# A transformer layer whose instruction order comes from a list scheduler in the kernel's source instead of hand-set slots

## The chip, the cores and the metric

The kernel runs on one core of a Trainium2 chip. The metric is the device time of one execution in microseconds (us), as the median of several runs. A core has TensorE (PE, matrix products; its weight loads are shown as PEld), VectorE (DVE), ScalarE (ACT), GpSimd (POOL) and SyncE (SP), whose queue issues most transfers here. Each engine works through its own queue in order. An instruction waits at the head of its queue until what it needs has come from the other engines, and everything behind it waits too. So the order in which the kernel's source emits instructions is the order in which each engine runs them.

## The reference

One layer, all in float32, with 512 tokens, width 2048, and 16 heads of 128 columns:

```
h    = RMSNorm(x)
proj = h @ w_in                      # 2048 x 8192: qA kA vA gA qB kB vB gB, 1024 columns each
A (8 heads): stick-breaking attention, strictly causal, weights from exp, log and a running sum
B (8 heads): softmax over the chunk itself and all chunks before it, normed q and k, bias by distance
mixed = concat(yA * silu(gA), yB * silu(gB))
x     = x + mixed @ w_out            # 2048 x 2048
```

## The kernel before

*Products.* Each matrix product is split twice. Every float32 operand is written as a high part plus a low part of a shorter format (`wh`, `wl` for weights, `xh`, `xl` for activations), and three matmuls (`three`, L217 to L219) give high x high, high x low and low x high. On top of that, a 2 x 2 scheme of blocks with seven products instead of eight (the names in `ORDER`: A11, A12, s3, A22, s2, s1, s4) is used; the operands' sums are made beforehand and the results are put together afterwards by `combine`.

*Units and steps.* The projection is 32 units (`u`). Four units make a group `g` of two heads: q, k, v and the gates. Even groups belong to attention A, odd ones to B. A unit has 4 steps, each with 7 products of 6 matmuls. The output product has 4 quarters of 512 columns, each with 8 steps, and a step has 7 products of 3 matmuls for each of two halves of the tokens (`a`). So there are 160 steps of 42 matmuls. The first eight steps alternate between units 0 and 1.

*What a step needs.* `load` issues two transfers of 256 KB for its weights (three buffers `wt`), `add` makes the sums on VectorE (L145 to L147: 512, 256 and 256 columns), `split` casts the high part on ScalarE (L157) and subtracts for the low part on VectorE (L159), in two parts of 1,024 and 768 columns with two buffers each. The activations go the same way in eight blocks `j` (`x_load`, `x_scale`, `x_sums` at L199 to L202, `x_split` with L210 and L213): once at the start for x, and once more for the mixed heads ahead of the output product. Their staging buffers are the pairs (`cq`, `ck`) and (`cv`, `cg`), which otherwise hold a group's q, k, v and gates.

*PSUM.* It has eight banks of 512 columns, and each product takes half a bank. The units go round five of the banks; banks 5, 6 and 7 (`SPARE`) serve the attention. `combine` reads a unit's seven products (L275 on ScalarE; L278, L279, L281, L282, L284 on VectorE) into `c`, or in the output stage into `co`. It has one scratch buffer `U`. In the output stage the halves `a` use banks 0 to 3 and 4 to 7.

*Attention.* For each head: `prep_a`, or `forth` and `back`, prepare q and k; `score` makes the scores of four blocks of tokens; `turn` transposes the weights (L574); `v_turn` transposes v (L601); `values` multiplies and then, with the head's gates, stores the mixed head to DRAM (`mixd`, L640). `gates` applies SiLU (L647), which needs a table to be loaded. `rstd` and `R` hold the row norms of x, made from sums of squares over `xs` (L316).

*What sets the order.* Time in the source is counted in slots, one for each product of a projection step. `at(slot, fn)` enters a job, `run(slot)` emits all that are due. A job is a generator whose `yield 1.5` means that it goes on 1.5 slots later; `TO_PE` (4 slots) and `TO_OTHER` (1.5) are the lags put between one engine's work and the next one's. `plan(g)` enters a group's jobs at fixed slots after the end of its units. The main loop emits the products in order, calling `run` between them, and the four parts of `combine` directly behind the second, fifth, sixth and seventh product of a unit's last step:

```
run(s0 + p - 0.5)
product(n, name)
if last and p in (1, 4, 5, 6):
...
    next(cg_, None)
run(s0 + p)
```

*Residual.* At the end of each quarter and half, two transfers bring the block of x (`xres`, L774), VectorE adds it to `co` (L780), and two transfers write the result (L782).

Of the kernel before, what the change touches and what calls it, by code (L numbers as in the profile page):

```python
# [14 lines left out]
P = 128  # L15
# [31 lines left out]
def trunk_kernel(ctx: ExitStack, tc: tile.TileContext, xT, xn, wi, wqk, wo, ng, qg, kg, rel, out):  # L47
# [55 lines left out]

    sequence = list(range(NU))
# [19 lines left out]

    wt_, whl = {}, {}

    def load(n):
        if n >= NS:
            return
# [10 lines left out]
    def add(n):  # L140

        if n >= NS:
            return
        t = wt_[n]
        dve.tensor_tensor(out=some(t, 8, -7, 2), in0=some(t, 5, -5, 2), in1=some(t, 1, 0, 2), op=ALU.add)  # L145
        dve.tensor_tensor(out=some(t, 9, 2), in0=some(t, 8, 2), in1=some(t, 0, 2), op=ALU.add)  # L146
        dve.tensor_tensor(out=some(t, 12, 1), in0=some(t, 9, 2), in1=some(t, 4, 2), op=ALU.add)  # L147

    def split(n, part):

        if n >= NS:
            return
        t = wt_[n][:, (0, 8 * P)[part]:(8 * P, 14 * P)[part]]
        w = (8 * P, 6 * P)[part]
        h, l = (tmp([P, w], f"{x}{part}", f"{x}{part}_{n}", F32R, bufs=2) for x in ("wh", "wl"))
        whl[n, part] = h, l
        act.copy(h, t)  # L157
        yield 1.5
        dve.tensor_tensor(out=l, in0=t, in1=h.bitcast(F32), op=ALU.subtract)  # L159
# [13 lines left out]
    stage = {}  # L173

    def x_load(j, mixed, tags):
        r = tmp([P, 4 * H], tags[0], f"xr{j}{mixed}")
        t = tmp([P, 4 * H], tags[1], f"xt{j}{mixed}")
        stage[j] = r, t
        if mixed:
            for tag in tags:  # L180
                emptied(tag, NG - 1)
        if mixed:
            a, b = mixd[NJ + j], mixd[j]
        else:
            a, b = xT[:, j, :], xT[:, j + NJ, :]
        sp.dma_start(r[:, :H], a[:, :H])
        sp.dma_start(r[:, H:3 * H], b)
        sp.dma_start(r[:, 3 * H:], a[:, H:])

    def x_scale(j):  # L190
        r, _ = stage[j]
        a, b = ng_t[:, j:j + 1], ng_t[:, j + NJ:j + NJ + 1]
        for s_, g_ in ((slice(0, H), a), (slice(3 * H, 4 * H), a), (slice(H, 3 * H), b)):
            act.activation(r[:, s_], r[:, s_], AF.Copy, scale=g_)

    def x_sums(j, eng):
        r, t = stage[j]
        two = lambda x: x.rearrange("p (a b) -> p a b", b=H)
        eng.tensor_tensor(out=two(t[:, :2 * H]), in0=r[:, None, 3 * H:].to_broadcast([P, 2, H]),  # L199
                          in1=two(r)[:, 0:3:2, :], op=ALU.subtract)  # L200
        eng.tensor_tensor(out=t[:, 2 * H:3 * H], in0=t[:, :H], in1=r[:, 2 * H:3 * H], op=ALU.subtract)
        eng.tensor_tensor(out=t[:, 3 * H:], in0=t[:, 2 * H:3 * H], in1=r[:, H:2 * H], op=ALU.add)  # L202

    def x_split(j):
        r, t = stage.pop(j)
# [3 lines left out]
        for src, a, b in ((r[:, :3 * H], 0, 3), (t, 3, 7)):  # L209
            act.copy(f(h[:, a:b]), src)  # L210
        yield 1
        for src, a, b in ((r[:, :3 * H], 0, 3), (t, 3, 7)):
            dve.tensor_tensor(out=f(l[:, a:b]), in0=src, in1=f(h[:, a:b]).bitcast(F32), op=ALU.subtract)  # L213
# [20 lines left out]

    def product(n, name, a=0):
        u, r = steps_[n]
        if u < NU:
            o = halves[:, place(unit_banks(u), name), :]
# [7 lines left out]
        else:  # L246
            o = halves[:, place((4 * a, None), name), :]
# [3 lines left out]
                  r == NJ - 1, skip_group_check=True)  # L251

# [18 lines left out]
    def combine(b, c, ut):  # L271


        u = ut.rearrange("p (a b) -> p a b", b=H)
        act.copy(u, pair(b, "A11", "A12"))  # L275
        yield
        c = c()
        dve.tensor_tensor(out=c[0][:, 1, :], in0=one(b, "s2"), in1=u[:, 0, :], op=ALU.add)  # L278
        dve.tensor_tensor(out=c[0][:, 0, :], in0=u[:, 0, :], in1=u[:, 1, :], op=ALU.add)  # L279
        yield  # L280
        dve.tensor_tensor(out=u, in0=pair(b, "s3", "s1"), in1=twice(c[0][:, 1, :]), op=ALU.subtract)  # L281
        dve.tensor_tensor(out=c[1], in0=pair(b, "A22", "s1"), in1=twice(u[:, 0, :]), op=ALU.add)  # L282
        yield
        dve.tensor_tensor(out=c[0][:, 1, :], in0=one(b, "s4"), in1=u[:, 1, :], op=ALU.subtract)  # L284

    def emptied(tag, g):

        n = head(g, 1)
        k = ("cq", "ck", "cv", "cg").index(tag)
        last = (("prep", n, 0), ("prep", n, 1), ("v", g, 1) if g < NG - 2 else ("mix", g, 1), ("mix", g, 1))[k]  # L290
        assert g < 0 or last in done, (tag, g)

    def result(u):
        emptied(("cq", "ck", "cv", "cg")[u % 4], u // 4 - 1)
        C[u // 4, u % 4] = t = tmp([P, 2, S], ("cq", "ck", "cv", "cg")[u % 4], f"c{u}")
        t = t.rearrange("p a (b c) -> p a b c", c=H)
        return [t[:, 0], t[:, 1]]


    def rsqrt(v, y, n):  # L300

        w = nwt[:, :n]
        act.activation(w, v, AF.Ln)
        act.activation(y, w, AF.Exp, scale=-0.5)
        yield 1
        dve.tensor_tensor(out=w, in0=y, in1=y, op=ALU.mult)
        dve.tensor_tensor(out=w, in0=w, in1=v, op=ALU.mult)
        dve.tensor_scalar(out=w, in0=w, scalar1=-0.5, scalar2=1.5, op0=ALU.mult, op1=ALU.add)
        dve.tensor_tensor(out=y, in0=y, in1=w, op=ALU.mult)

    def x_stats(t, i):
        k, = yield from buffer("W")
        x_ = tmp([P, S], "W", "xs", bufs=3)
        sp.dma_start(x_, xn[t][:, i * S:(i + 1) * S])
        yield 7
        act.activation(x_, x_, AF.Square, accum_out=ssx[:, t * 4 + i:t * 4 + i + 1])  # L316
# [3 lines left out]
    def x_rstd():  # L320
        yield from until(lambda: all(("stat", t, i) in done for t in range(NT) for i in range(4)))
        dve.tensor_reduce(out=vx, in_=ssx.rearrange("p (a b) -> p a b", b=4), axis=mybir.AxisListType.X, op=ALU.add)
        dve.tensor_scalar(out=vx, in0=vx, scalar1=1.0 / D, scalar2=EPS, op0=ALU.mult, op1=ALU.add)
        yield 1
        yield from rsqrt(vx, rstd, NT)
        dve.tensor_tensor(out=rstd2, in0=rstd, in1=rstd, op=ALU.mult)
        yield from x_spread()

    def x_spread():
# [4 lines left out]
        pool.memset(o, 1.0)  # L334
        for t in range(NT):
            dve.tensor_scalar(out=d[:, t * P:(t + 1) * P], in0=ident, scalar1=rstd[:, t:t + 1], scalar2=None, op0=ALU.mult)
        yield 2
        for t in range(NT):
            s_ = slice(t * P, (t + 1) * P)
# [481 lines left out]
```

## Time and profile before

| | |
|---|---|
| median of 3 runs | 1125.21 us (1120.92 to 1125.61) |
| the profiled execution | 1127.8 us, span 1126.0 us |
| busy: PE / DVE / ACT / POOL | 981.1 / 895.8 / 582.8 / 8.3 us |
| granted TensorE clock, mean | 0.961 |
| matmuls | 7,496, of which 6,720 are the 160 steps' |
| bytes moved | 112.42 MB, 100 GB/s over the span |

Busy time is the union of an engine's instructions. Matmuls overlap one another, and their ends are modelled, so a busy PE may still do less than it can; counting the matmuls that start in a stretch is safer. In a table of windows, each row is a stretch of the span with its length, and for each engine the busy time and the number of instructions; then the granted clock (PEclk, 1 is full speed), the share of the DMA engines' time, and GB/s. A row of waits has who waited, for whom, then the total in us, the number of waits, and the longest. A row of the timeline has start and duration in us, engine, source line, operation, result and sources, and in brackets the engine's idle time before it with what ended that.

### The profile page before, as it was taken

To read this page: it belongs to the slowest core of one execution; us is meant where nothing else is said; L and a number is where in the kernel's file an instruction comes from. 1 tells how busy PE (TensorE), PEld (TensorE's weight loads), DVE (VectorE), ACT (ScalarE), POOL (GpSimd) and SP (SyncE) were. 2 spreads that over 40 slices of the span, in tenths; PEclk is the share of its full clock that TensorE was granted. 3 is DMA by queue.
4 is the path that set the end of the run, shared out by engine and by line. 5 is a ranking of instruction groups with operands and counts; after the bars stand their busy time and mean duration, and the time that the engine had idled before them with its cause. 6 is when DMAs were issued, how large, how long until landed. Compare 5 with 4: busy or idle time off the path is not lost. (4 is left out here: it accounts for less than half of the span.)

```text
span 1126.0 us, 19319 instructions
## 1 busy us (share of the span) xinstructions
PE 981.1 (87%) x7496; PEld 945.5 (84%) x7496; DVE 895.8 (80%) x1541; ACT 582.8 (52%) x1073; POOL 8.3 (1%) x49
## 2 busy tenths in 40 slices
PE   4678879999998899999899999998998888797986
PEld 4568879998998899889889998898898887697986
DVE  6778968787887878888878887887778799867775
ACT  5665654465365545653655565455556454332331
POOL 0000000000000000000000000000000000000000
PEclk9789999999998999999899999999899999899998
DMA  4462223222222322223223222322123244434341
GB/s 149 147 204 80 76 66 112 92 88 85 85 76 76 94 86 94 85 85 103 64 77 115 95 86 83 104 76 85 58 75 103 85 134 143 146 115 147 110 153 57
DMA packets 63884, 112.42 MB, mean 100 GB/s; under 512 B 7472, under 2 KB 11568, under 8 KB 63792
## 3 DMA queue, kind: packets, MB, share of 16 engines
q1 hardware_dynamic: 63792, 111.19, 30.9%
q8 instruction: 58, 0.95, 0.4%
q14 instruction: 34, 0.28, 0.1%
HBM read 102.77 MB, written 8.39 MB: 99 GB/s over the span
## 5 line engine op out<-in xcount | busy, mean ns | idle before, releaser
L217 PE MATMUL banks<-xh,wh 128*128 128x256 f32 x1792 | 528.6, 295 | 44.5 <-DVE c L278 21.0
L219 PE MATMUL banks<-xh,wl 128*128 128x256 f32 x1792 | 518.7, 289 | 35.8 <-DVE wl L159 35.7
L218 PE MATMUL banks<-xl,wh 128*128 128x256 f32 x1792 | 515.8, 288 | 1.1 <-DVE xl L213 1.1
L157 ACT CAST wh<-wt 128x1024 fp32r<-128x1024 f32 (+1 forms) x320 | 295.1, 940 | 365.0 <-DVE wt L147 124.1
L159 DVE TENSOR_TENSOR wl<-wt,wh 128x1024 fp32r<-128x1024 f32 (+1 forms) x320 | 343.8, 1088 | 106.4 <-ACT wh L157 105.7
L217 PEld LDWEIGHTS banks<-xh,wh 128*128 128x128 f32 x1792 | 352.8, 197 | 53.9 <-DVE c L278 27.3
L219 PEld LDWEIGHTS banks<-xh,wl 128*128 128x128 f32 x1792 | 352.4, 197 | 41.2 <-DVE wl L159 41.2
L218 PEld LDWEIGHTS banks<-xl,wh 128*128 128x128 f32 x1792 | 352.5, 197 | 1.8 <-DVE xl L213 1.4
L217 PE MATMUL banks<-wh,xh 128*128 128x256 f32 x448 | 131.6, 294 | 18.3 <-DVE co L278 9.7
L218 PE MATMUL banks<-wl,xh 128*128 128x256 f32 x448 | 132.4, 296 | 7.5 <-DVE wl L159 7.5
L219 PE MATMUL banks<-wh,xl 128*128 128x256 f32 x448 | 131.6, 294 | 3.2 <-DVE xl L213 3.2
L145 DVE TENSOR_TENSOR wt<-wt 128x512 f32<-128x512 f32 x160 | 109.5, 684 | 0.0
L217 PEld LDWEIGHTS banks<-wh,xh 128*128 128x128 f32 x448 | 89.8, 200 | 20.7 <-DVE co L278 11.4
L218 PEld LDWEIGHTS banks<-wl,xh 128*128 128x128 f32 x448 | 89.8, 201 | 10.5 <-DVE wl L159 10.5
L219 PEld LDWEIGHTS banks<-wh,xl 128*128 128x128 f32 x448 | 90.0, 201 | 5.3 <-DVE xl L213 5.2
L146 DVE TENSOR_TENSOR wt<-wt 128x256 f32<-128x256 f32 x160 | 68.0, 425 | 5.5
L147 DVE TENSOR_TENSOR wt<-wt 128x256 f32<-128x256 f32 x160 | 68.1, 425 | 5.5
L574 PE MATMUL banks<-ident,W 128*128 128x128 f32 x160 | 30.1, 288 | 12.9 <-DVE wtl L582 5.3
L275 ACT COPY U<-banks 128x512 f32<-128x512 f32 x40 | 23.5, 588 | 31.5 <-PE banks L219 21.3
L580 ACT CAST wth<-banks 128x128 fp32r<-128x128 f32 (+1 forms) x64 | 26.8, 423 | 22.0 <-PE banks L574 22.0
L281 DVE TENSOR_TENSOR U<-banks,c 128x512 f32<-128x512 f32 x32 | 22.1, 690 | 19.6 <-PE banks L219 19.6
L582 DVE TENSOR_TENSOR wtl<-banks,wth 128x128 fp32r<-128x128 f32 (+1 forms) x64 | 30.6, 483 | 7.1 <-ACT wth L580 7.0
(112 smaller groups left out, 902.7 us busy)
## 6 DMA issues: line engine op xcount, KB each, us to landing
wt<-in_wi SPq DMA_DIRECT2D x256, 256.0 KB, 3.0
wt<-in_wo SPq DMA_DIRECT2D x64, 256.0 KB, 3.1
xs<-in_xn SPq DMA_DIRECT2D x16, 256.0 KB, 4.0
mixd<-c SPq DMA_DIRECT2D x16, 256.0 KB, 2.1
xres<-in_xn SPq DMA_DIRECT2D x16, 256.0 KB, 3.9
out<-xres SPq DMA_DIRECT2D x16, 256.0 KB, 2.6
xr<-in_xT SPq DMA_DIRECT2D x16, 128.0 KB, 3.5
xr<-in_xT SPq DMA_DIRECT2D x8, 256.0 KB, 3.8
```

The source lines that it names most:

```text
L145: dve.tensor_tensor(out=some(t, 8, -7, 2), in0=some(t, 5, -5, 2), in1=some(t, 1, 0, 2), op=ALU.add)
L146: dve.tensor_tensor(out=some(t, 9, 2), in0=some(t, 8, 2), in1=some(t, 0, 2), op=ALU.add)
L147: dve.tensor_tensor(out=some(t, 12, 1), in0=some(t, 9, 2), in1=some(t, 4, 2), op=ALU.add)
L157: act.copy(h, t)
L159: dve.tensor_tensor(out=l, in0=t, in1=h.bitcast(F32), op=ALU.subtract)
L217: pe.matmul(o, lh, rh, start=start, stop=False, **kw)
L218: pe.matmul(o, lh, rl, start=False, stop=False, **kw)
L219: pe.matmul(o, ll, rh, start=False, stop=stop, **kw)
L275: act.copy(u, pair(b, "A11", "A12"))
L574: pe.transpose(t[:, j * P:(j + 1) * P], src[:, j * P:(j + 1) * P], ident)
L580: act.copy(th[:, blocks, :], tv)
L582: dve.tensor_tensor(out=tl[:, blocks, :], in0=tv, in1=th[:, blocks, :].bitcast(F32), op=ALU.subtract)
```

## The change

The slots, lags and the loop over them are removed. In their place a list scheduler runs while the kernel's source is executed. It keeps a clock of its own and a queue of ready operations for each engine. An operation has an engine, a cost (constants such as 0.075 us + 1.04 ns for each column on VectorE), and a due time. Each job is a generator that yields either an operation, which is made ready when its inputs are finished by that clock (0.06 us later, or 0.4 us for TensorE), or a condition to wait for. When an engine is free, the ready operation with the earliest due time is emitted. TensorE takes ready attention work first and the next product of the steps (0.705 or 0.355 us) otherwise, when the weights' split, the activations and the bank are there. The operations for weights and activations are due a few us ahead of the product that uses them (`need`). Loads have a bandwidth of 330 GB/s and a latency of 2.2 us in this model.

```diff
+    def issue(engine, op):
+        op.fn()
+        busy[engine] = clock[0] + op.cost
...
+    def schedule(next_product):
...
+            for e in ready:
+                if busy[e] > clock[0] + 1e-9:
+                    continue
+                if ready[e]:
+                    k = min(ready[e], key=lambda k: (k[0].due(), k[3]))
...
+                elif e == "PE":
+                    op = next_product()
...
+    def sums(n, k0, k1):
...
+        yield DV(512, lambda: dve.tensor_tensor(out=some(t, 8, -7, 2), ...), need(k0, 4))
+        spawn(split(n, 0, k0), (0, n))
...
+        yield AC(w, hi, need(k, 2.6))
+        h, l = x
+        yield DV(w, lambda: dve.tensor_tensor(out=l, in0=t, in1=h.bitcast(F32), op=ALU.subtract), need(k, 0.5))
...
-    def give(i, wait=3.0):
-        yield wait * LAG[0]
+    def give(i):
         del owner[i]
-    LAG = [1.0]
-    TO_PE, TO_OTHER = 4.0, 1.5
```

The transfers and operations are the same but for these points. The mixed activations' block `j` is staged in (`cq`, `ck`) where `j` is even and in (`cv`, `cg`) where it is odd, each block after the one before it in its pair; before, blocks 0 to 3 all used (`cq`, `ck`). `cv` comes free when the last group's heads are mixed, `cg` when the second of them is stored:

```diff
+        tags = STAGE[j % 2]
...
+            yield lambda: (("store", g, j % 2) in done and ("store", g + 1, j % 2) in done
+                           and all(emptied(t_, NG - 1) for t_ in tags)
+                           and position[0] >= at_step[steps_.index((last, j // 2))] + NP)
```

The steps of the output stage take the halves `a` in turn, product by product, but for the last step of a quarter, which does half 0 and then half 1; the first two steps of the first quarter run half 0 of both, then half 1 of both. A product may start when both halves of its bank have been read (`holder`). `combine` is a job of its own, whose parts become ready as the products finish and are due 0.5 to 3 us later. The residual of the first three quarters is added by a transfer that accumulates into `co`, issued by GpSimd; the store follows at least 5 us later in the plan. In the last quarter VectorE adds it from a buffer that is loaded when the last head is mixed:

```diff
+    def residual(u, a, co, h, rows_, qs):
+        op = G(1.2, lambda: pool.dma_start(co[:, h, :], xn_rows(rows_)[:, qs], accum_op=ALU.add))
+        yield op
+        later_ = clock[0] + 5.0
+        later(later_, lambda: None)
+        yield lambda: clock[0] >= later_ - 1e-9
+        yield L_(P * 2048, lambda: sp.dma_start(out[rows_, qs], co[:, h, :]))
...
+            yield DV(256, lambda: dve.tensor_tensor(out=w1, in0=w1, in1=xf[0][:, 1], op=ALU.subtract), soon(1))
+            yield DV(256, lambda: dve.tensor_tensor(out=c[0][:, 0], in0=c[0][:, 0], in1=xf[0][:, 0], op=ALU.add), soon(3))
+            yield DV(512, lambda: dve.tensor_tensor(out=c[1], in0=c[1], in1=xf[1], op=ALU.add), soon(3))
```

`forth` and `back` become one job, `prep_b`, which keeps one bank for both transposes. The attention of group `g` no longer starts at set slots: `prep_a` or `prep_b` starts when the unit is combined, `score` when q and k are ready, and so on, limited by the same three banks and the same buffers (`L`: 1, `W`: 3).

More of the change, by code (lines that the diff above doesn't have):

```diff
@@ L101, in trunk_kernel, with later, __init__ @@
     sp.dma_start(ng_t, ng)
+    clock = [0.0]
+    events, ready, waiting = [], dict(PE=[], DVE=[], ACT=[], POOL=[], SP=[]), []
+    busy = dict.fromkeys(ready, 0.0)
+    dma_free = [0.0]
+    count = [0]
+    done = set()
+    def later(t, fn):
+        count[0] += 1
+        heapq.heappush(events, (t, count[0], fn))
+    class Op:
+        def __init__(self, engine, cost, fn, due=None, lag=0.0):
+            self.engine, self.cost, self.fn, self.lag = engine, cost, fn, lag
+            self.due = due if callable(due) else (lambda d=clock[0] + LATE if due is None else due: d)
@@ new lines, in trunk_kernel, with DV, AC, M @@
+    LATE = 5.0
+    def DV(w, fn, due=None, n=1):
+        return Op("DVE", (0.075 + 1.04e-3 * w) * n, fn, due)
+    def AC(w, fn, due=None, n=1):
+        return Op("ACT", (0.085 + 0.85e-3 * w) * n, fn, due)
+    def M(cost, fn):
+        return Op("PE", cost, fn, 0.0)
+    def G(cost, fn, due=None):
+        return Op("POOL", cost, fn, due)
+    def L_(nbytes, fn, due=None):
+        return Op("SP", 0.15, fn, due, lag=nbytes)
+    def advance(gen, rank):
+        r = next(gen, None)
+        if r is None:
+            return
+        if isinstance(r, Op):
+            wait = 0.4 if r.engine == "PE" else 0.06
+            later(clock[0] + wait, lambda: ready[r.engine].append((r, gen, rank, count[0])))
+        else:
+            waiting.append((rank, r, gen))
@@ L289, in emptied @@
         k = ("cq", "ck", "cv", "cg").index(tag)
[L290 to L297, printed above, removed]
+        return g < 0 or (("read", n, 0), ("read", n, 1), ("c_v", g), ("store", g, 1))[k] in done
@@ L300, in rsqrt @@
     def rsqrt(v, y, n):
         w = nwt[:, :n]
[L303 to L316, printed above, removed]
+        yield lambda: "nwt" not in done
@@ L409, in qk_of @@
         n = head(g, h)
-        yield from until(lambda: n == 0 or all(("score", n - 1, b) in done for b in range(NT)))
+        yield lambda: n == 0 or ("scores", n - 1) in done
         if n not in qk:
@@ new lines, in score @@
+        yield lambda: all(("prep", n, k) in done for k in range(2)) and (n == 0 or ("scores", n - 1) in done)
+        for b in range(NT):
+            i = None
+            if g % 2 == 0:
+                i, = yield from buffer("L")
+            else:
+                yield lambda: n in bias
+            k, = yield from buffer("W")
+            z_ = yield from take(("score", n, b))
+            w = P * (b + 1)
+            L = tmp([P, S], "L", "L")[:, :w] if g % 2 == 0 else None
+            W = tmp([P, S], "W", "W", bufs=3)[:, :w]
+            yield M(0.15 + 0.35 * max(256, w) / 256, lambda: scores(banks[:, z_, :], n, b, g % 2 == 0))
+            z = banks[:, z_, :w]
+            spawn(score_a(n, b, z_, z, L, W, w, i, k) if g % 2 == 0 else score_b(n, b, z_, z, W, w, k), (n, 1))
@@ L475, in trunk_kernel, with prep_b @@
     rq = single([P, 2, 2, NT], "rq")
-    def forth(g, kind, h):
-        yield from until(lambda: not h or all(("prep", head(g, 0), k) in done for k in range(2)))
-        l_of[g, kind, h], = yield from buffer("L")
+    def prep_b(g, kind, h):
+        n = head(g, h)
+        yield lambda: "R" in done and ("unit", 4 * g + kind) in done
+        yield lambda: all(("read", n - 1, k) in done for k in range(2)) if h else kind == 0 or ("read", n, 0) in done
+        yield lambda: not h or kind == 0 or ("read", n, 0) in done
+        k, = yield from buffer("L")
         t_ = tmp([P, S], "L", "tm")
@@ L501, in forth @@
[L501 to L523 removed]
+        yield DV(4, lambda: dve.tensor_tensor(out=y, in0=y, in1=rstd, op=ALU.mult))
@@ L525, in load_bias @@
+        give(i)
+        done.add(("prep", n, kind))
     def load_bias(g, h):
@@ L643, in gates @@
+        done.add(("store", g, h))
     def gates(g):
+        yield lambda: "R" in done and ("unit", 4 * g + 3) in done
         f = C[g, 3]
[L645 to L654 removed]
@@ L788 @@
+    for j in range(NJ):
+        spawn(activations(j, 1), (2 * NG, j))
+    for a in range(2):
+        spawn(residual_load(a), (2 * NG, 0))
+    schedule(next_product)
+    assert not waiting and position[0] == len(program), (position, [w[0] for w in waiting], owner, live)
 def kernel(x, norm_g, w_in, q_norm_g, k_norm_g, rel_bias, w_out):
```

779 lines of the change are left out of this document (423 added, 356 removed).

## The prediction

> **What bounds the kernel now.** I read the whole span by stage first. The stages were cut where the first matmul of a step falls: eight steps of start-up, steps 8 to 127 of the projection in five pieces, then the four quarters of the output stage.
>
> ```profile
> core 0 of [0], span 1126.0 us
> core 0: us, PE busy (x) PEld busy (x) DVE busy (x) ACT busy (x) POOL busy (x), PEclk, DMA share, GB/s
> 0.00:90.80 90.80, 52.42 (x337) 50.12 (x338) 65.14 (x95) 55.70 (x95) 1.85 (x11) 0.87 0.51 162
> 90.80:148.90 58.10, 51.43 (x402) 49.57 (x402) 50.41 (x90) 32.74 (x63) 0.35 (x2) 0.99 0.23 74
> 148.90:364.30 215.40, 197.16 (x1539) 190.88 (x1538) 173.57 (x308) 116.89 (x227) 1.69 (x10) 0.98 0.27 86
> 364.30:577.80 213.50, 197.60 (x1538) 191.16 (x1537) 173.37 (x309) 116.08 (x226) 1.69 (x10) 0.98 0.27 87
> 577.80:788.90 211.10, 194.86 (x1539) 188.36 (x1538) 173.22 (x309) 115.99 (x226) 1.83 (x11) 0.99 0.28 89
> 788.90:909.30 120.40, 108.16 (x808) 103.71 (x807) 93.97 (x186) 68.67 (x150) 0.84 (x5) 0.94 0.26 85
> 909.30:971.50 62.20, 49.71 (x338) 44.62 (x338) 59.41 (x89) 30.79 (x34) 0.00 (x0) 0.95 0.43 137
> 971.50:1020.70 49.20, 44.02 (x338) 43.22 (x337) 35.70 (x55) 15.90 (x18) 0.00 (x0) 0.93 0.41 125
> 1020.70:1069.50 48.80, 42.88 (x339) 42.08 (x339) 35.80 (x55) 15.91 (x18) 0.00 (x0) 0.97 0.40 131
> 1069.50:1126.00 56.50, 42.84 (x338) 41.83 (x336) 35.22 (x54) 14.14 (x16) 0.00 (x0) 0.91 0.33 106
> sum 1126.00, PE 981.09 PEld 945.55 DVE 895.83 ACT 582.81 POOL 8.26; mean PE 98.11 PEld 94.55 DVE 89.58 ACT 58.28 POOL 0.83
> ```
>
> TensorE leads almost everywhere, VectorE is close behind, DMA is never over 0.51. Only in 909.3 to 971.5 does VectorE fill its stage (59.4 of 62.2 us). Five short stretches, same columns, give the unit prices:
>
> ```profile
> 1007.96:1013.00 5.04, 5.04 (x45) 5.04 (x44) 3.55 (x5) 1.88 (x3) 0.00 (x0) 1.00 0.30 109
> 663.50:670.92 7.42, 7.28 (x61) 6.95 (x59) 7.32 (x14) 4.38 (x8) 0.00 (x0) 1.00 0.40 120
> 944.30:951.35 7.05, 6.08 (x44) 5.27 (x43) 6.91 (x12) 3.56 (x4) 0.00 (x0) 1.00 0.47 140
> 173.30:175.70 2.40, 0.15 (x2) 0.00 (x0) 2.40 (x5) 0.63 (x1) 0.14 (x1) 1.00 0.19 72
> 177.30:180.70 3.40, 3.40 (x18) 3.40 (x18) 3.16 (x7) 0.82 (x2) 0.00 (x0) 0.50 0.27 99
> ```
>
> The first is one undisturbed step: 42 product matmuls start in it (the 45 count those that overlap its edges) in 5.04 us, 0.12 us each. The second is a step with 16 attention matmuls in it: 2.38 us more, 0.149 us each. The third is VectorE packed solid: one block of activations (sums and split) and one of weights in 7.05 us, 3.52 us a block; their 5,632 columns make it 1.25 ns a column. The last two show that a gap costs twice: TensorE stood 2.4 us, and from 1.6 us later the granted clock was 0.50 for 3.4 us.
>
> So 160 steps need 806 us, and 776 further matmuls (7,496 less 6,720) about 116. Some 204 us of the span is neither. By stage, time less floor is: start-up 90.8 - 40.3 = 50; the five projection pieces 7.8, 25, 23, 21 and 20, in all 97; the quarters 22, 8.9, 8.5 and 16. I asked next which waits make up TensorE's share in the projection (the first four and the last of its 18 rows, together 68 us), at the start, and in the output stage:
>
> ```profile
> PE banks L217 <- DVE c L278: 17.4, 25, 2.3
> PE banks L219 <- DVE wl L159: 15.0, 18, 1.5
> PE banks L217 <- DVE c L282: 9.7, 6, 2.1
> PE banks L601 <- DVE wtl L582: 5.5, 3, 2.3
> ...
> PE banks L438 <- DVE wtl L582: 0.2, 1, 0.2
> ```
> ```profile
> PE banks L219 <- DVE wl L159: 20.6, 6, 5.9
> PE banks L217 <- ACT wh L157: 11.9, 1, 11.9
> ```
> ```profile
> PE banks L217 <- DVE co L278: 9.7, 8, 2.9
> PE banks L217 <- ACT wh L157: 7.7, 3, 2.8
> PE banks L218 <- DVE wl L159: 7.5, 9, 2.3
> ```
>
> The largest wait is a matter of order alone. Two products of a unit share a PSUM bank; the combination's read of `s2` (L278) is put ahead of the product `s1`, whose write to that bank then waits:
>
> ```profile
> 626.42 0.43 DVE L278 TENSOR_TENSOR c<-banks,U 128x256 f32<-128x256 f32 x1 [1.01 <-PE banks L219]
> ...
> 626.90 0.39 PE L217 MATMUL banks<-xh,wh 128*128 128x256 f32 x1 [0.59 <-DVE c L278]
> ```
>
> **The change, part by part.** No matmul is added or removed, so the floor stays. What moves is the order on each queue, so the sum goes by stages, against this execution's 1127.8 us (span 1126.0), 2.6 us above the median of the runs, 1125.21.
>
> Start-up (90.8 us). The first matmul comes at 11.9. VectorE needs 16 blocks at 3.52 (8 of activations, 8 of weights), 56 us, two combinations of 1,792 columns at 1.25 ns, 4.5, and begins about 6 us in: a floor of about 69 with TensorE's last step behind it. Now it is busy 65.1 of 90.8, as the hand order keeps an activation block in its in-order queue while weights that TensorE waits for (20.6 us) lie behind it. Ordering by due time can go to 69 at most; I take half of the 22 us, rounded up: -13, ends -22 and +5 (the loads of the statistics, 16 of 256 KB, now go by due time between those of the weights).
>
> Projection (818.5 us, 97 above its floor). The new code emits the combination's first read only when the model has `s2` finished, and by then `s1` is issued: the waits on L278 and L282, 27 us, should go. What is late next: the read itself now waits for `s1`, one product of 0.72 us, and stands at the head of VectorE's queue; over 30 units 22 us of VectorE, which has room there (173 of 213 us, 0.81). Waits for weights (15.0): splits go by need instead of by slot, half, -7.5. Waits of the attention's own matmuls (the row of 5.5 and those after it but one, 25 of the 68): some go with the order by readiness, but the hand lags of 1.5 to 4 slots, which covered most of them, go too; -5. The 97 less the waits' 68 leaves 29 for the half clock and its like, which go with the gaps; in proportion to 39.5 of 68 that would be 17, and I take half, as new gaps come: -9. In all -48; ends -80 (17 left of 97, 0.09 us for each attention job) and +17 (L278's waits kept and the attention's doubled, less the weights).
>
> Hand-over to the output stage. Blocks 0 to 3 of the mixed activations went through one pair of buffers, before the last gates were ready. Now odd blocks go through the pair (cv, cg), which comes free only with the last store of the last group, and the program asks for block 1 as its second step:
>
> ```profile
> 914.78 1.28 ACT L647 ACT_TABLE_LOAD   x1
> 916.08 1.06 ACT L647 ACTIVATE c<-c 128x1024 f32<-128x1024 f32 x1
> ```
> ```profile
> mixd<-c SPq DMA_DIRECT2D x16, 256.0 KB, 2.1
> xres<-in_xn SPq DMA_DIRECT2D x16, 256.0 KB, 3.9
> ...
> xr<-mixd SPq DMA_DIRECT2D x16, 128.0 KB, 3.5
> ```
>
> From the last projection matmul: combination's end 1.6; gates 1.3 (1,024 columns); table and SiLU 2.4; two products of 512 columns 1.3; store 2.1 and its issue 0.5; load 3.5 and three issues 1.5; sums, cast, subtraction 3.6: 18 us. TensorE has 2.5 us of work meanwhile, so it stands some 15 us and starts again at half clock (about +2). In return the even blocks are done early and VectorE no longer fills the stage: 18 + 37.8 (the other steps) + 2 + 3 (the boundary below) is 61, against 62.2. I take -2, ends -8 and +15 (odd blocks one after the other: 8.6 us each, under the 10.1 of two steps, so hidden unless late).
>
> Quarter boundaries. Each of quarters 1 and 2 is 8.5 to 8.9 above its 40.3. The residual's loads were issued at the end and VectorE waited for them with weights behind it; that and the bank order are the output stage's first three waits. Now the plan alternates the halves `a`, the sums leave VectorE (12 of 16 adds of 0.69 us) for 12 accumulating transfers on POOL's queue, which had 8.3 us of work. POOL waits for `co` with nothing behind it that the output stage needs. SP's stores wait for the accumulation, with weight loads queued behind them: the plan puts them 5 us later, the loads 7 us ahead of need. No row shows an accumulation; the nearest are the store's 2.1 and the plain load's 3.9, and reading both sides one after the other would be 6.0. I take 3.9, hidden; at 6.0 SP stands 1 us, still inside the 7. What stays is VectorE's peak: two steps' weights, 7.0, and two combinations, 4.5, in 10.1 us, and the one buffer `U` that both halves share, about 3 us. So -5 each, -10, ends -14 and 0.
>
> Last quarter, 16 above its floor: its start as above, -3.5. At its end:
>
> ```profile
> 1118.77 0.41 DVE L284 TENSOR_TENSOR co<-banks,U 128x256 f32<-128x256 f32 x1
> 1120.61 0.69 DVE L780 TENSOR_TENSOR xres<-co,xres 128x512 f32<-128x512 f32 x1 [1.42 <-DMA xres<-in_xn]
> ```
>
> Two adds follow L284 after a wait of 1.42; they end at 1122.3. The new tail has its residual early and three adds of 1,024 columns (1.3) ahead of the last subtraction, which would end at 1120.5: -1.8. With the bank wait of `s1` some -6, ends -9 and +2. Sum: -13 - 48 - 2 - 10 - 6 = -79; 1127.8 - 79 = 1049, at the median's level **1046**.
>
> On the clock, the Trainium skill, page "TensorE: Matmul & The Clock Gate", Part 1, has the half clock come after an idle window of about 3.4 us. Here 2.4 us idle were enough (173.3 to 175.7). By that rule the gaps of 1 to 2.6 us in the projection would cost no clock, the -9 would fall away, and the sum would be 1055; the trace decides.
>
> **Rivals.** *Near the floor.* Every excess goes but what VectorE forces: -22 - 80 - 8 - 14 - 9 = -133, 993. For it: TensorE's floor and VectorE's 888 us fit beside each other. Against: at 993 VectorE would be 0.89 busy in an in-order queue.
> *VectorE gives it back.* At 1046 it is (895.8 - 8)/1049 = 0.85 busy. If its blocked 0.7 us per unit lands on the weights, the projection keeps only half, -24, start-up -5, the rest -5: 1091. For it: the hand-over stage, where VectorE sets the pace as soon as it is full.
> *The plan runs dry (slower).* The attention puts 193 jobs on TensorE's in-order queue (12 per head, 16 heads, and one). The hand lags kept them off it until their inputs were old; the new plan has them wait 0.4 us in a model. Each that comes to the head d us early stops all products behind it: 193 d. At d = 0.41 the 79 are eaten; at 0.45, 1133. Against it: in the projection such waits come to 25 us now, 0.13 a job.
> *No difference.* The gaps only move, since both engines were near full: 1125.
>
> **How the numbers follow.** Forecast 0.53 (1015 to 1080), near the floor 0.08, VectorE 0.22, slower 0.12, none 0.05. Faster is 0.53 + 0.08 + 0.22 = 0.83; 0.5% (5.6 us) is about what a measurement of this kernel tells from no change. Below 995 lies a fifth of the second case (0.02), above 1115 the last two (0.17): the range is 995 to 1115.
>
> **What would show it.** Waits of TensorE on the combination's first add near 0 instead of 17.4 and 9.7 us; eight projection units in about 200 us with the granted clock at 0.99 or over; step 8 before 82 us; one gap of 12 to 16 us with half clock behind it at the first output step; quarters of about 44 us; VectorE near 0.85. Wrong would make it: many TensorE waits of 0.3 to 1 us at transposes and scores; VectorE idle at combinations while weights are late; SP waiting for an accumulation for longer than 5 us.

## The result, and the profile after

The changed kernel takes 1027.08 us (median; 1025.13 to 1029.22) against 1125.05 for the kernel before on the same chip. The ratio is 0.9137, with an interval of 0.9108 to 0.9165. The forecast was 1046, in a range of 995 to 1115.

The profiled execution took 1026.74 us. These are its windows, cut where the same steps begin as in the prediction's table (start-up; the projection in five pieces; the four quarters of the output stage), with the same columns:

```profile
0.00:76.60 76.60, 51.65 (x336) 48.71 (x336) 64.18 (x108) 55.89 (x98) 1.83 (x11) 0.89 0.60 193
76.60:123.00 46.40, 46.36 (x385) 46.00 (x384) 45.21 (x76) 29.60 (x54) 0.00 (x0) 1.00 0.29 92
123.00:322.20 199.20, 193.32 (x1561) 189.48 (x1560) 171.04 (x317) 122.37 (x239) 1.99 (x12) 1.00 0.30 93
322.20:517.70 195.50, 189.60 (x1538) 186.14 (x1537) 168.42 (x309) 118.91 (x230) 1.64 (x10) 1.00 0.30 95
517.70:711.80 194.10, 189.64 (x1539) 186.27 (x1538) 168.70 (x309) 118.83 (x231) 1.78 (x11) 1.00 0.30 97
711.80:814.80 103.00, 99.84 (x806) 97.66 (x805) 91.53 (x184) 69.73 (x150) 0.84 (x5) 1.00 0.32 102
814.80:881.80 67.00, 45.70 (x338) 44.12 (x337) 52.80 (x83) 29.52 (x32) 0.00 (x0) 0.80 0.41 130
881.80:926.40 44.60, 40.83 (x338) 40.42 (x337) 32.86 (x51) 16.14 (x19) 3.67 (x4) 1.00 0.51 144
926.40:970.90 44.50, 40.84 (x338) 40.43 (x337) 32.93 (x51) 16.16 (x19) 3.50 (x4) 1.00 0.51 142
970.90:1025.00 54.10, 41.00 (x338) 40.39 (x336) 32.30 (x52) 14.12 (x17) 3.51 (x4) 0.95 0.36 98
sum 1025.00, PE 938.78 PEld 919.63 DVE 859.97 ACT 591.28 POOL 18.76; mean PE 93.88 PEld 91.96 DVE 86.00 ACT 59.13 POOL 1.88
```

Set against the table before, stage by stage:

| stage | before | after | moved | forecast |
|---|---|---|---|---|
| start-up | 90.8 | 76.6 | -14.2 | -13 |
| projection | 818.5 | 738.2 | -80.3 | -48 |
| hand-over (quarter 0) | 62.2 | 67.0 | +4.8 | -2 |
| quarters 1 and 2 | 98.0 | 89.1 | -8.9 | -10 |
| last quarter | 56.5 | 54.1 | -2.4 | -6 |
| sum | 1126.0 | 1025.0 | -101.0 | -79 |

Four fifths of the gain are in the projection, which now stands 17 us above its floor instead of 97. The clock column reads 1.00 in all of it. These are TensorE's waits there, the whole list:

```profile
PE banks L374 <- DVE c L515: 9.4, 13, 1.0
PE banks L374 <- DVE c L508: 4.3, 4, 1.1
PE banks L374 <- DVE U L513: 2.9, 3, 1.1
PE banks L838 <- ACT W L744: 1.2, 2, 1.0
PE banks L374 <- DVE st L815: 1.0, 2, 0.5
PE banks L838 <- ACT W L822: 0.2, 1, 0.2
```

It comes to 19 us, where 68 stood. No wait for weights is left, and the attention's own (the last three rows) are 2.4 us instead of some 25. Three rows, 16.6 us, are products that wait until a combination has read their bank.

One reason why weights are no longer late is seen on VectorE. The first fence has VectorE's waits in the projection of the kernel before, the second those of the changed kernel; L508, L513 and L515 are the lines that were L278, L281 and L282:

```profile
...
DVE c L278 <- PE banks L219: 27.1, 15, 3.0
DVE U L281 <- PE banks L219: 17.6, 23, 0.9
...
DVE c L284 <- PE banks L219: 6.7, 6, 1.5
```
```profile
...
DVE c L508 <- PE banks L376: 5.0, 6, 1.3
...
DVE c L515 <- PE banks L376: 3.2, 3, 1.3
...
DVE U L513 <- PE banks L376: 0.2, 1, 0.2
```

Before, the combination stood at the head of VectorE's queue for 51.4 us in all, waiting for products that were not finished, with weights and attention work behind it. Now it is 8.4 us. The scheduler makes each part ready only when its product is finished in its model, and that model was close enough to the chip for it. That this is what brings the weights in time is not shown: in one of the experiments below (the split early alone), 35.7 us of such waits are left on VectorE and TensorE waits for no weights either. Putting the splits earlier in the queue was enough there.

### The profile page after: what moved, and what is told of

It is laid out like the page before. It is cut to its first block, busy times and chain, and to the rows that moved or that the text cites. A ratio compares the mean times of both kernels' runs of the same rounds, so it can differ in the third digit from the quotient of the medians.

```text
span 1025.0 us, 19307 instructions
## 1 busy us (share of the span) xinstructions
PE 938.8 (92%) x7496; PEld 919.6 (90%) x7496; DVE 860.0 (84%) x1531; ACT 591.3 (58%) x1082; POOL 18.8 (2%) x61
## 4 chain that ended last, share of the span: by engine, by line
PE 74%; DVE 14%; ACT 5%; issue 3%; DMA 3%; SPq 1%; DVEq 0%; ACTq 0%
PE banks L374 24%; PE banks L375 23%; PE banks L376 23%; DVE wl L303 3%; ACT wh L298 2%; PE banks L838 2%; DVE U L513 2%; DVE wt L282 1%; DVE xl L358 1%; DMA wt<-in_wi 1%; PE banks L766 1%; DVE c L515 1%; DMA xcv<-in_xT 1%; ACT xh L357 1%; DVE wt L286 1%
## 5 line engine op out<-in xcount | busy, mean ns | idle before, releaser
L374 PE MATMUL banks<-xh,wh 128*128 128x256 f32 x1792 | 521.8, 291 | 32.4 <-ACT wh L298 11.8
L376 PE MATMUL banks<-xh,wl 128*128 128x256 f32 x1792 | 510.1, 285 | 1.0 <-DVE wl L303 1.0
L298 ACT CAST wh<-wt 128x1024 fp32r<-128x1024 f32 x320 | 300.6, 942 | 309.3 <-PE banks L375 171.3
L303 DVE TENSOR_TENSOR wl<-wt,wh 128x1024 fp32r<-128x1024 f32 x320 | 347.6, 1089 | 86.8 <-ACT wh L298 85.1
L374 PEld LDWEIGHTS banks<-xh,wh 128*128 128x128 f32 x1792 | 346.3, 193 | 39.4 <-DVE c L515 12.9
L375 PEld LDWEIGHTS banks<-xl,wh 128*128 128x128 f32 x1792 | 346.6, 193 | 10.4 <-DVE xl L358 10.1
L376 PEld LDWEIGHTS banks<-xh,wl 128*128 128x128 f32 x1792 | 346.5, 193 | 1.2 <-DVE wl L303 1.2
L282 DVE TENSOR_TENSOR wt<-wt 128x512 f32<-128x512 f32 x160 | 109.6, 687 | 25.0 <-DMA wt<-in_wo 16.2
L375 PE MATMUL banks<-wl,xh 128*128 128x256 f32 x448 | 128.3, 286 | 0.0
L374 PEld LDWEIGHTS banks<-wh,xh 128*128 128x128 f32 x448 | 87.6, 196 | 32.0 <-ACT xh L357 15.6
L739 DVE TENSOR_TENSOR_SCAN W<-L,W 128x128 f32<-128x128 f32 (+3 forms) x32 | 26.3, 821 | 0.0
```

The lines of the kernel that those rows point to most:

```text
L282: yield DV(512, lambda: dve.tensor_tensor(out=some(t, 8, -7, 2), in0=some(t, 5, -5, 2), in1=some(t, 1, 0, 2), op=ALU.add), need(k0, 4))
L298: act.copy(x[0], t)
L303: yield DV(w, lambda: dve.tensor_tensor(out=l, in0=t, in1=h.bitcast(F32), op=ALU.subtract), need(k, 0.5))
L374: pe.matmul(o, lh, rh, start=start, stop=False, **kw)
L375: pe.matmul(o, lh, rl, start=False, stop=False, **kw)
L376: pe.matmul(o, ll, rh, start=False, stop=stop, **kw)
```

## The experiments

**The order of one read, and when the weights are split, in the old kernel.** Two reorderings that the hand-set plan could have had: the read of `s2` goes behind the product `s1`; and the sums and splits of weights that the plan has during a unit's last step (those of the second step after it) are no longer put off by 3.9 slots.

```diff
 # "s2 read late", in the main loop (and the same in the output stage)
-                if last and p in (1, 4, 5, 6):
+                if last and p in (1, 5, 6):
+                    if p == 5:
+                        next(cg_, None)
 # "split early"
-late = 3.9 if r == (NR if proj else NJ) - 1 else 0
+late = 0
```

*The s2 read late alone.*

> The kernel before with one thing changed: the combination's read of s2 is put behind the product s1 instead of ahead of it (in the projection and in the output stage). My theory: TensorE's waits on L278 (17.4 us in the projection, 9.7 us in the output stage) are a matter of order and go to under 3 us together, with some of the half clock behind them: 1125 - 27 + a few us that VectorE now stands waiting for s1 = about 1100 us. Rival: VectorE, which now waits 0.7 us longer at each combination with weights behind it, gives it back as later waits for weights: 1118 us or more.

It took 1134.28 us, 1.009 of before (1.0073 to 1.0107): 0.9% slower, clear of the noise. The theory fell, and the time is where its rival had it. The first two rows of TensorE's waits in the projection of this kernel, then VectorE's waits for the combination:

```profile
PE banks L219 <- DVE wl L159: 17.3, 19, 1.7
PE banks L217 <- DVE c L282: 15.6, 6, 3.4
```
```profile
DVE c L278 <- PE banks L219: 36.7, 24, 3.2
...
DVE c L284 <- PE banks L219: 7.6, 6, 1.7
```

The 17.4 us on L278 are gone from TensorE's list, as meant, and other rows grew: weights from 15.0 to 17.3, the next combination's read from 9.7 to 15.6. VectorE's wait at L278 grew from 27.1 to 36.7 us, but the 17.6 at L281 are gone, as one wait now serves both reads: VectorE stands 44.3 us at the combination, less than the 51.4 before. So the rival's mechanism, a VectorE that is held longer, is not borne out, and why the waits moved is open. TensorE's whole list is 72 us in 61 waits where 68 in 77 stood: fewer and longer ones. What grew most is the half clock, 61.4 us of this projection against 38.7 before. At half clock the products start 0.21 us apart instead of 0.12, so 22.7 us more of it is worth an estimated 10 us, as much as the loss.

*The split early alone.*

> The kernel before with the extra 3.9 slots set to 0 alone, the combination's read of s2 still ahead of the product s1. It completes the square: before 1125, order alone 1134, both 1082. Theory (the two need each other): with the weights' sums and splits ahead of it on VectorE's queue, the combination's read comes later, and the product s1 waits for it longer in each of 40 combinations; the waits for weights go, those on L278 grow from 27 us to 45 or more: 1105 to 1125 us. Rival (the weights' lateness alone was the cost, the order is worth nothing): 1080 to 1090 us.

1103.7 us, 0.9807 (0.9774 to 0.9841). TensorE's waits in the projection:

```profile
PE banks L217 <- DVE c L278: 37.0, 26, 3.8
```

The time is just below the theory's 1105 to 1125. The waits for weights are gone, and the wait behind the combination's read has doubled: splits now stand ahead of that read in VectorE's queue.

*Both.*

> As b_order, and the extra 3.9 slots by which the sums and splits of weights were put off in the last step of a unit are set to 0. Theory: these slots make the waits for weights at the first product of a unit's second step (15.0 us in the projection, 7.5 in the output stage); half of that goes: about 10 us under b_order. Rival: with the weights ahead of the combination on VectorE's queue the combination is late, and the next unit's products wait for banks: the same as b_order or slower.

1082.26 us, 0.962 (0.9595 to 0.9646). So, against 1125.05, the four corners are 0, +9, -21 and -43 us (beside these runs the kernel before took 1123.4 and 1123.6, so each is good to some 2 us): the first edit loses 9 by itself and wins 21 on top of the second. With both, half clock is down to 30.7 us and VectorE stands 24.3 us at the combination. Two small moves in the old plan are worth 43 us, where the scheduler is worth 98; so much can be had by order alone. TensorE's waits in the projection show what the hand plan could not shed with them:

```profile
PE banks L217 <- DVE c L282: 17.9, 6, 5.0
PE banks L574 <- DVE wtl L582: 14.8, 11, 3.1
```

The next product still waits for the combination's read, and the attention's transposes wait for the operation that makes the low parts of its weights. Both still go by slots.

**Readiness without due times.** Ready operations are taken in the order in which they became ready:

```diff
-k = min(ready[e], key=lambda k: (k[0].due(), k[3]))
+k = min(ready[e], key=lambda k: k[3])
```

> The changed kernel, but each engine of the plan takes its ready operations in the order in which they became ready; due times are not used. Theory: the due times are what puts a unit's weights, its combination and the attention in the right order on VectorE's queue, as the two runs on the kernel before say; without them waits for weights and for the combination come back, at the start too: 1045 to 1070 us. Rival: the order by readiness, with products filling TensorE, does it all: within 6 us of 1027.

1045.63 us, 0.9298 (0.927 to 0.9327): 18.5 us above the changed kernel, 79 below the kernel before. The projection lost 11.7 and the hand-over 4.7 of it. TensorE's waits in the projection:

```profile
PE banks L374 <- DVE c L515: 16.3, 17, 1.7
```

Weights, which the theory had expected to be late, are not on the list. What came later is the combination's read, 16.3 us where 9.4 stood; a read that has lost its due time lies behind every split that became ready before it. VectorE's own wait at the combination stays short, 6.8 us in all, so it is the readiness rule and not the due times that keeps it so. Due times are worth about a fifth of the gain (18.5 of 98 us); four fifths are there without them.

**The lag ahead of TensorE.** Attention work is put on TensorE's queue 0.4 us after its inputs are finished in the model. Without it, and with five times as much:

```diff
-wait = 0.4 if r.engine == "PE" else 0.06
+wait = 0.0 if r.engine == "PE" else 0.06   # the other kernel: 2.0
```

> The changed kernel, but the plan makes TensorE's attention work ready 0.0 us after its inputs instead of 0.4 us. The slower rival of the prediction, a plan that runs dry: each of 193 jobs comes up to 0.4 us earlier against its inputs, up to 77 us in all: 1050 us or more. Theory: an input is seen by TensorE within 0.1 us of its engine's end in the trace, and the plan holds 0.1 us for that anyway, so waits stay near the 2 us of now: 1022 to 1034 us.

> The changed kernel, but 2.0 us instead of 0.4 us, close to what the hand-set lags held. Theory: TensorE fills the time with products, so lags as such cost little; the attention only ends later, in the hand-over: 1025 to 1040 us. Rival: cutting the lags was the gain of the projection; then half of its 80 us goes, 1060 us or more.

With 0.0: 1038.84 us, 0.9225 (0.9184 to 0.9265), between theory and rival. With 2.0: 1023.33, 0.9104 (0.9073 to 0.9134), whose interval overlaps that of 0.4. The first two rows of TensorE's waits in the projection with 0.0:

```profile
PE banks L374 <- DVE c L515: 11.6, 17, 1.0
PE banks L838 <- ACT W L822: 6.8, 15, 0.7
```

Without the lag the attention's multiplies wait for their weights, 6.8 us in 15 waits where 0.2 stood; that is half of the 12 us lost, all of it in the projection (749.8 us). With 2.0 the list holds the three rows of the combination alone, 7.6, 7.1 and 4.3 us, and no attention wait is left. The projection's profile is 6.3 us shorter, but 24 attention matmuls (3.6 us at 0.149) have slid into the first output step. So the lag is a guard against the model's error, needed but with little depending on its size above 0.4. That a gain of the change lies in lags as such, the rival, fell.

**The hand-over.** Blocks 0 to 3 are staged in (`cq`, `ck`) again, one after the other, as before the change:

```diff
-tags = STAGE[j % 2]
+side = 0 if mixed and j < 4 else j % 2     # also in the lock "stage"
+tags = STAGE[side]
```

> The changed kernel, but blocks 0 to 3 of the mixed activations are staged in (cq, ck) again, as before the change. Theory: the first output step lasts 30.7 us because block 1 waits for the last group's gates and stores, and 27 us at half clock follow; with blocks 0 to 3 done ahead the hand-over stage goes from 67.0 to 50 to 54 us: about 1012 us. Rival: VectorE sets this stage (52.8 of 67.0 us busy; before the change it was full and the stage took 62.2): at most 5 us, 1022 us.

1019.95 us, 0.9075 (0.9061 to 0.909), 7 below the changed kernel. The hand-over takes 60.8 us instead of 67.0 and its first step 11.8 instead of 30.7. Some of that came back as steps of 10 to 13 us later in the stage, where blocks arrive singly; hence the place between the theory's number and the rival's. The staging part of the change is a loss. With the last quarter's residual loads put off as well, so that they no longer stand ahead of the mixed blocks on SP's queue:

```diff
-yield lambda: ("mix", NG - 1, 1) in done
+yield lambda: ("mix", NG - 1, 1) in done and position[0] >= at_step[steps_.index((NU + 1, 2))]
```

> a_stage, with the four loads of the last quarter's residual put off to the second quarter; now they stand on SP's queue ahead of the mixed blocks and two steps of weights at the hand-over (1.85 us of issue, then weights issued at 834.2). Theory: block 3 and the weights come 2 us earlier and the stall of steps 131 and 132 (13 us over two steps) loses 2 to 5 us: 1015 to 1018. Rival: that stall is the chain of five blocks through one pair of buffers, each with 3.5 us of VectorE work: no change, 1019 to 1021.

1016.82 us, 0.9044 (0.901 to 0.9077), as the theory had it; the hand-over is 56.5 us in its profile. The two edits together are clear of the noise; the second alone, 3 us, is not, as its interval overlaps that of the first.

**The one scratch buffer of the output stage.** Each half gets its own `U`:

```diff
-x.append(tmp([P, S], "U", "U")...
+x.append(tmp([P, S], ("U", "U1")[a], "U")...   # and a lock for each half
```

> The changed kernel with a scratch buffer U of its own for the second half of the output stage. Theory: the shared buffer is what makes the 4 us at each of three quarter starts (TensorE waits for ScalarE's copy to U 6.2 us, for the combination L515 4.9 us) and ScalarE's copy waits 4.8 us for it in the tail: 3 x 3 us and 2 to 3 us at the end: about 1015 us. Rival: VectorE's peak there, two combinations and two steps of weights, 11.5 us in 10, sets the quarter starts and the tail is its chain of adds: 3 us at most, 1024 us.

1026.77 us, 0.9134 (0.9115 to 0.9154): no change. TensorE's waits from the first output step on, of this kernel:

```profile
PE banks L374 <- DVE co L515: 7.2, 3, 2.6
```

The 6.2 us for ScalarE's copy into `U` are gone, and the wait for the last read of the same bank grew from 4.9 to 7.2, so 3.9 us less is waited at the three starts. A quarter's first step keeps its length all the same (8.8, 9.4 and 9.4 us, against 9.3, 9.2 and 9.2). The clock is part of why. Two windows at a quarter's start, of the changed kernel and then of this one:

```profile
883.10:886.50 3.40, 1.69 (x12) 1.49 (x12) 3.40 (x8) 0.59 (x1) 1.76 (x2) 1.00 0.49 70
886.50:889.90 3.40, 2.07 (x17) 2.07 (x18) 1.61 (x4) 0.70 (x1) 1.59 (x2) 1.00 0.92 222
```
```profile
884.40:887.80 3.40, 1.35 (x12) 1.14 (x11) 3.40 (x6) 0.00 (x0) 2.45 (x3) 1.00 0.44 72
887.80:891.20 3.40, 3.40 (x19) 3.40 (x18) 2.63 (x5) 1.04 (x1) 1.14 (x2) 0.50 0.77 117
```

In the changed kernel two gaps share two windows and both run at full clock. Here the one gap that is left falls in a single window, with 2.05 us idle, and the next window is at half; so it is at all three starts. So the second buffer takes a wait away and the half clock gives it back. VectorE is busy through the whole first window in both kernels; how long the start would be by that alone, at full clock, is not shown.

**The residual.** All four quarters as the last one: VectorE adds from a buffer loaded a quarter ahead, with no accumulating transfer:

```diff
-final = u == NU + 3
+final = out_
...
+for q in range(4):
+    yield lambda: q == 0 or ("xread", a, q - 1) in done
```

> The changed kernel, but VectorE adds the residual in all four quarters, from loads issued a quarter ahead, as the changed kernel does in its last one; no accumulating transfers. This parts the early load from the accumulation. Theory: the gain at the quarters (4.5 us each) is the early load and the order; the accumulation only takes 4 x 0.69 us of VectorE work a quarter away, which falls on the quarter starts where VectorE is full: 2 to 3 us for each of three, 1032 to 1038 us. Rival: hidden, since VectorE is idle later in each quarter: within 3 us of 1027. Second rival: the stores no longer wait for the accumulation on SP's queue, and weights come earlier: under 1024.

1048.05 us, 0.9316 (0.9291 to 0.9341): 21 us slower, more than any theory had. The kernel has another effect than the one it was made for. In that form of the combination the first half's store is put in its job ahead of the last subtraction, so `U` is held longer, and the other half's copy waits (ScalarE's row in the timeline, second quarter's start; read from the code and the trace, no run changes it alone):

```profile
891.82 0.59 ACT L489 COPY U<-banks 128x512 f32<-128x512 f32 x1 [7.14 <-DVE co L531]
```

Each later quarter starts with a step of 16 us instead of 9.2, with 6.8 us of half clock in it: 3 x 6.8 = 20 of the 21. What accumulation by itself is worth against VectorE's adds stays open. The reverse question, whether stores that wait for it hurt anybody, has an answer. With the store planned 9 us behind the accumulation instead of 5:

```diff
-later_ = clock[0] + 5.0
+later_ = clock[0] + 9.0
```

> The changed kernel with the store of a quarter planned 9 us instead of 5 us after the accumulating transfer, which lands after 6.2 us. Theory: SP's waits for the accumulation (15.8 us in 6) go, VectorE's waits for the weights behind them (16.2 us) shrink, and TensorE sees nothing, as it waits for no weights there now: 1024 to 1029 us. Rival: the late weights are what makes VectorE's peak at the quarter starts: 3 us a quarter, under 1020.

1028.19 us, 0.9142 (0.9118 to 0.9166): no change, though SP's wait for the accumulation is gone and VectorE waits 13.4 instead of 16.2 us for weights of the output stage. TensorE's waits stay as they were (6.4 and 4.9 us at the quarter starts, 6.2 and 4.9 before). One start did grow, the last, from 9.2 to 11.7 us, with 6.8 us of half clock behind a window with 1.9 us idle.

**The best version** has the old staging, the late residual loads and the lag of 2.0.

> a_defer with the 2.0 us of lag in front of TensorE's attention work from a_wait2, which took 6 us from the projection and gave some back in the output stage. If the two are independent the projection keeps its 6 us and the hand-over the gain of a_defer: about 1011 us. If the longer lag ends the last group's attention so late that the hand-over loses what the projection wins: 1016 us or more.

1013.24 us, 0.9005 (0.8983 to 0.9028), the fastest kernel here, some 14 us below the changed one and between the two times expected. What the lag adds on top of the other two edits, 3.6 us, is not clear of the noise.

## Why the prediction was right, and where its sizes were off

**Sign and order of size** came from the right stages: four of the five stage terms fell inside their own ends, and the projection, at -80.3, came out at its lower end of -80. That match is chance: the 17 us that this end leaves were meant for the attention's jobs, and the 17 left are waits for banks. What was to show it came as well: eight units in 199.2, 195.5 and 194.1 us at full clock, step 8 at 76.6, quarters of 44.6, VectorE at 860.0/1025 = 0.84. Only the combination's waits did not fall near 0.

**The projection, -48, was mis-sized, by its parts unevenly.** Waits for weights, "half, -7.5": all 15 went. The attention's own waits, -5: 22.6 of 25 went. "The half clock and its like", -9: all 29 went, nothing of the 17 us left being beyond the listed waits. "The waits on L278 and L282, 27 us, should go": 16.6 us of bank waits are still there, so 10.5 went. The four together, -7.5 too small, -17.6 too small, -20 too small and 16.5 too large, make up the 32 us of difference within some 4. Each of the first three was taken at less than the whole for a cost that did not come. Behind the weights stood "the read itself now waits for `s1`, one product of 0.72 us, and stands at the head of VectorE's queue; over 30 units 22 us of VectorE". All of the combination's waits measured 8.4 us, in the place of 51.4 us that VectorE had already stood there, which the trace of before shows and the sum leaves out. So VectorE's queue was cleared, not blocked. The attention's term was kept small because the hand lags go; 0.4 us of lag in their place was enough. The clock's was halved for new gaps; the longest in the list is 1.1 us.

The step that failed the other way is that the waits on the combination's reads should go. The new waits are where the prediction looked for none: a next product finds its bank not yet read. With a unit's five banks and a combination that is emitted as its products finish, the read is behind whatever VectorE has in hand; without due times, which let it pass, the largest of these waits was 16.3 us instead of 9.4.

**The clock.** The prediction took half of what "in proportion" would be 17; the share of half clock did not follow the waits. One row of the changed kernel, and then the hand-over's:

```profile
57.10:818.30 761.20, 736.08 (x5954) 722.00 (x5952) 666.25 (x1225) 473.29 (x917) 6.25 (x38) 1.00 0.30 96
818.30:845.60 27.30, 9.50 (x37) 8.33 (x38) 16.56 (x27) 7.04 (x7) 0.00 (x0) 0.50 0.43 135
```

With waits of 1.1 us at most, not one window of the 761 us was granted half clock (more on this in the last section). But the term of 29 was not all clock. The projection of the kernel before had 38.7 us of half clock, which at 0.21 us a product instead of 0.12 cost an estimated 17. What the other 12 were is not shown.

**Start-up, -13, came as -14.2** (half of the 22 us, which it says it takes, would be -11), by the cause named: waits for weights there, 20.6 us before, are down to the last row of TensorE's waits from the start to step 8, and activations take their place.

```profile
PE banks L374 <- ACT wh L298: 11.8, 1, 11.8
PE banks L375 <- DVE xl L358: 8.4, 7, 1.8
...
PE banks L376 <- DVE wl L303: 1.0, 1, 1.0
```

**The hand-over, -2, came as +4.8**: mechanism right, chain longer. Rows of the timeline of all engines, in order:

```profile
819.51 0.58 PE L374 MATMUL banks<-wh,xh 128*128 128x256 f32 x1 [3.87 <-DVE c L515]
...
820.37 1.22 DVE L924 TENSOR_TENSOR c<-c,R 128x1024 f32<-128x1024 f32 x1
...
821.62 1.06 ACT L927 ACTIVATE c<-c 128x1024 f32<-128x1024 f32 x1 [3.36 <-DVE c L924]
...
825.63 0.93 SPq L918 DMA_DIRECT2D mixd<-c  x2
826.66 1.86 SPq L570 DMA_DIRECT2D xres<-in_xn  x4
...
836.65 0.58 PE L374 MATMUL banks<-wh,xh 128*128 128x256 f32 x1 [13.57 <-ACT xh L357]
```

The last unit ended at 814.8. "Combination's end 1.6": the gates' multiply started 5.6 us later, as VectorE had the even blocks and weights in its queue. "Table and SiLU 2.4": the table was loaded meanwhile, so 1.1. "Its issue 0.5": 0.9, and four loads of the residual, 1.9, and an even block's loads, 1.4, stood between store and block. From 814.8 to the product at 836.65 it is 21.9 us where the prediction has 18. The stand was two gaps, 3.9 and 13.6, against "some 15", and the half clock lasted 27.3 us instead of a window: TensorE was busy for 45.7 us in this stage and for 40.8 in the next, 4.9 against "about +2".

**Quarters 1 and 2, -10, came as -8.9.** For the accumulation "I take 3.9" was too low: 6.2, slightly over the far bound of 6.0. Issues of transfers (KB each, us to landing), then SP's wait for it:

```profile
out<-co SPq DMA_DIRECT2D x16, 256.0 KB, 4.1
co<-in_xn POOLq DMA_DIRECT2D x12, 256.0 KB, 6.2
```
```profile
SPq L554 <- DMA co<-in_xn: 15.8, 6, 4.0
```

"At 6.0 SP stands 1 us": it stood up to 4.0, in 6 of 12. That it costs nothing held all the same, as the longer delay showed. What stays at a boundary are the two things that the prediction named, the peak of VectorE's work and the shared `U`. TensorE's waits from the first output step on:

```profile
...
PE banks L374 <- ACT U L489: 6.2, 3, 2.1
PE banks L374 <- DVE co L515: 4.9, 3, 1.6
...
```

These are the three boundaries, two waits at each and 11.1 us in all. That all three run at full clock was no part of the forecast; it hangs on how the gaps fall on the clock's windows, as the second buffer's kernel shows.

**The last quarter, -6, came as -2.4.** The -1.8 by which the last subtraction would end earlier did not come. The three adds are done early, but the way from the last matmul to the end is 9.7 us, against 8.5 before. VectorE's rows of the timeline at the end:

```profile
1017.32 0.42 DVE L508 TENSOR_TENSOR co<-banks,U 128x256 f32<-128x256 f32 x1 [0.73 <-ACT U L489]
...
1020.72 0.42 DVE L530 TENSOR_TENSOR co<-banks,U 128x256 f32<-128x256 f32 x1
```

Half 1's combination starts behind half 0's and VectorE is packed from there, at 0.42 and 0.69 us an operation. A second `U` took away the 0.73 and brought the end no closer.

**The rivals.** "VectorE gives it back" failed, as VectorE stood 8.4 us at the combination and not 22 more; a busy share of 0.84, as foreseen, was no bound. "The plan runs dry" needed 0.41 us for each of the 193 jobs: it measured 2.4/193 = 0.01, and even with no lag at all about 0.04. "Near the floor" came true in the projection alone (by its own sum it is 992, not 993).

## What to carry to other kernels

Read the waits of the second-busiest engine too: what stands at the head of its in-order queue for a product that isn't finished delays all behind it. One reordering can lose by itself (+9 us) and win on top of another (-21 us), so try such edits in pairs, and read the clock beside the waits: with the second buffer the half clock took back what the waits gave. The scheduler without due times kept about four fifths of its gain, and a lag of a few tenths of a us ahead of the busiest queue pays for the model's error. A hand-over chain through DRAM wants its queues clear: the old staging and four late loads were together worth 10 us here.

## What the runs showed of the hardware

The granted clock changes on a fixed grid of 3.41 us, and how much of one such window TensorE was idle goes with the clock of the next. Two windows of the kernel before, one after the other:

```profile
412.80:416.20 3.40, 1.30 (x9) 1.09 (x9) 2.14 (x4) 0.00 (x0) 0.00 (x0) 1.00 0.45 154
416.20:419.60 3.40, 3.40 (x18) 3.40 (x17) 1.87 (x4) 0.21 (x1) 0.00 (x0) 0.50 0.02 5
```

With 2.1 us idle the next window is at half. Of the windows of before that ran at full clock (from 20.3 us, where its record of the clock begins), all 17 with 1.9 us or more of idle time were followed by half clock, and none with less. A window already at half was followed by another with as little as 0.5 us idle (from 795.1). Over the other traces it is no sharp line: between some 1.3 and 1.9 us windows went either way. The changed kernel's quarter starts, with 1.7 us idle in the window shown with the second buffer, keep full clock, and this window of the kernel with the late read, with 1.3 idle, is followed by half:

```profile
253.60:257.00 3.40, 2.09 (x13) 1.32 (x12) 3.40 (x4) 1.96 (x5) 0.00 (x0) 1.00 0.00 0
```

So a gap of 2 us is free or costs a window at half speed by where it falls on the grid. In the projection of the changed kernel no window has more than 1.2 us idle, which fits the clock loss going as a whole. The Trainium skill, page "TensorE: Matmul & The Clock Gate", Part 1, has such a free-running window of 3413 ns, and the grid agrees; it puts the half clock after at least one idle window, and here 0.4 to 0.56 of one was enough. By that rule the clock's part of the prediction's term would have been 0; it came to an estimated -17.

The other unexpected number is the accumulating transfer's 6.2 us for 256 KB, beside 4.1 for the plain store of the same tile. It was issued by GpSimd and the store by SP, so how much of the difference is the adding is not shown.
